# A transformer layer on one core: the feed-forward part started step by step of its contraction

## The chip, the cores and the metric

The kernel runs on one core of a Trainium2 chip. The metric is the device time of one execution in microseconds. A core has five engines, each with an instruction queue of its own that runs in order: TensorE (PE in the profile) multiplies matrices, VectorE (DVE), ScalarE (ACT) and GpSimd (POOL) work elementwise, SyncE (SP) issues DMAs; ACT issues DMAs here as well. Data lies in HBM (DRAM scratch arrays end in `_scr`), in SBUF (128 partitions) and, as matmul results, in eight PSUM banks.

## The reference

One layer over 2048 tokens of width 1024. A mixer (latent attention and a state-space part side by side) gives `y_lat`; then the feed-forward part, with d_ff = 2816:

```
x = layer_norm(DN_ALPHA * x + g1 * y_lat, ln1_g, ln1_b)
u = layer_norm(x) * (1 + sc2) + sh2                      # modulate
gate, up = split(u @ w_gate_up)                          # 1024 -> 2 x 2816
f = (silu(gate) * up) @ w_down                           # 2816 -> 1024
x = layer_norm(DN_ALPHA * x + g2 * f, ln2_g, ln2_b)
```

All of it is float32.

## The kernel before

**Precision.** A float32 product is three matmuls (`mm3`, L63 to L65): each operand is split into a rounded high part `hi` (a cast, `hi_of` L53 or an ACT copy) and the rest `lo` (`lo_of` L58, a subtraction), and hi·hi, hi·lo and lo·hi are added up in one PSUM bank.

**Stages.** Inputs and projections, attention, the `Out` stage (output product, first layer norm, second norm, and a turn that puts tokens on the free axis), then the feed-forward part: gate and up from about 1887 us, down from about 2776 us, and the end at 3318.

**Out** walks over 16 tiles of 128 tokens in time slots. For a tile: L1433 adds the residual (`xo`, DVE), statistics (L1409, DVE), L1439 normalises (ACT), L1440 and L1441 scale and shift (POOL), statistics again, L1451 makes the second norm `no` (ACT), eight transposes (L1461, PE) and eight ACT copies (L1464, `u2o`) that apply scale and shift, and a DMA to `u2_scr`. The order inside `Out` is written out by hand; after its end a scheduler merges what follows by its own costs.

**Gate and up** is one level of Strassen-Winograd: seven products in place of eight. A block is one of 22 slices f of d_ff for one of two token halves b: 7 products x 4 contraction steps k x 3 matmuls = 84 matmuls. `tokens(b)` prepares the token operands B11, B12, B21, B22 and their combinations T1 to T4 for k = 0 to 3: four loads from `u2_scr` (L1582), four DVE combinations (L1583 to L1586), seven hi casts (L1551, ACT) and seven lo (L58, DVE). They stay in SBUF for 22 blocks, as 28 pairs `oh`/`ol`. `weights(f)` does the same for one slice of weights (A11 to A22, S1 to S4): casts on POOL (L53), lo and combinations (L1565 to L1568) on DVE. `block(b, f)` runs product after product, four k each, and evacuates banks between them.

**Down** takes the tokens in four quarters q, the output columns in two halves. `hidden(q)` loads the 22 hidden slices (`hraw`, DMAs on ACT's queue, L1638) and splits them (hi on POOL). `down` runs 22 x 4 tiles x 3 matmuls per half, its weights loaded on SP and split on POOL and DVE. `add` and `finish` apply g2, the residual and the last norm; for q < 3 half of `finish` is on POOL (L1683, L1684).

The pairs `oh`/`ol` of `tokens` and `hidden` share one pool of 28, and the weights of products 0 to 3 have one buffer each, so a later use waits for PE's last read of the earlier one.

Of the kernel before, what the change touches and what calls it, by code (L numbers as in the profile page):

```python
# [10 lines left out]
F32 = mybir.dt.float32  # L11
# [1200 lines left out]
def preload(tc, E, rawp):  # L1212
    nc = tc.nc
    P = nc.gpsimd
    I = E.I
    E.after = ExitStack()
# [3 lines left out]
    E.wg = [(wp.tile([128, S5W], F32R, name="glh%d" % k), wp.tile([128, S5W], F32R, name="gll%d" % k)) for k in range(4)]  # L1220
# [93 lines left out]

class Out:
    def __init__(self, tc, E):

        self.tc, self.E = tc, E
        nc = self.nc = tc.nc
        I = E.I  # L1320
        self.cp = E.after.enter_context(tc.tile_pool(name="ou_c", bufs=2, side="right", reuse_waits="tile"))
        rows = E.after.enter_context(tc.tile_pool(name="ou_g", bufs=1, side="right", reuse_waits="tile"))
        self.att, self.s5, self.loaded = {}, {}, {}
        E.wo.append((rows.tile([128, D], F32R, name="woh7"), rows.tile([128, D], F32R, name="wol7")))
        self.operands(0)
        for k in range(4):
            self.att_load(0, k)
            self.att_part(0, k)
        self.rows = rows
        self.sh2 = rows.tile([128, 8], F32, name="sh2")  # L1330
        nc.sync.dma_start(self.sh2, E.mod_scr[1].rearrange("(k p) -> p k", p=128))
        self.sc2 = rows.tile([128, 8], F32, name="sc2")
        nc.sync.dma_start(self.sc2, E.mod_scr[2].rearrange("(k p) -> p k", p=128))
        nc.vector.tensor_scalar(self.sc2, self.sc2, 1.0, None, ALU.add)
# [46 lines left out]
    def run(self):  # L1381
# [66 lines left out]
        def second_end(t, m):  # L1448
# [19 lines left out]
        def slot(t):  # L1468
# [26 lines left out]
            turns = {2: [], 3: [0], 4: [1], 5: [2, 3]}.get(t, [b] if mb else [])  # L1495
# [35 lines left out]

class FeedForward:
    def __init__(self, tc, E, wp):

        self.tc, self.nc, self.E, self.I, self.wp = tc, tc.nc, E, E.I, wp
        self.wgu = E.I["w_gate_up"][0].rearrange("(k p) n -> p k n", p=128)

    def pair(self, pool, name, bufs=None):

        hi = pool.tile([128, 512], F32R, name=name + "h", bufs=bufs)  # L1540
        lo = pool.tile([128, 512], F32R, name=name + "l", bufs=bufs)
        return hi, lo

    def wpair(self, i):

        return self.pair(self.wp if i < 4 else self.wq, "w" + PRODUCTS[i][1], 1)

    def split(self, eng, t, raw):
# [5 lines left out]
        lo_of(self.nc.vector, lo, raw, hi)  # L1554

    def weights(self, f):
# [3 lines left out]
        r = {n: self.wp.tile([128, 512], F32, name="wraw", bufs=8) for n in ("A11", "A21", "A22", "A12", "S1", "S2", "S3", "S4")}  # L1560
# [8 lines left out]
        for _, n, _ in PRODUCTS:  # L1569
            self.split(P, w[n], r[n])  # L1570
        return w

    def tokens(self, b):

        nc, V = self.nc, self.nc.vector
        u = {n: [self.pair(self.op, "o") for _ in range(4)] for _, _, n in PRODUCTS}
        for k in range(4):
            r = {n: self.tp.tile([128, 512], F32, name="uraw", bufs=8) for n in ("B11", "B12", "B22", "B21", "T1", "T2", "T3", "T4")}
            for n in ("B11", "B12", "B22", "B21"):
# [3 lines left out]
            V.tensor_tensor(r["T1"], r["B12"], r["B11"], ALU.subtract)  # L1583
            V.tensor_tensor(r["T2"], r["B22"], r["T1"], ALU.subtract)
            V.tensor_tensor(r["T3"], r["B22"], r["B12"], ALU.subtract)
            V.tensor_tensor(r["T4"], r["T2"], r["B21"], ALU.subtract)  # L1586
            for _, _, n in PRODUCTS:
                self.split(nc.scalar, u[n][k], r[n])
        return u

    def block(self, b, f, w, u):

        nc, V, P = self.nc, self.nc.vector, self.nc.gpsimd
        tp = self.tp
# [22 lines left out]
        u3 = tp.tile([128, 512], F32, name="u3")  # L1617
        V.tensor_tensor(u3, bank["b"], s1, ALU.add)
        c22 = tp.tile([128, 512], F32, name="c22")
# [4 lines left out]
        col = b * 1024  # L1624
        nc.scalar.dma_start(self.E.h_scr[f * 128:(f + 1) * 128, col:col + 512], g1)
# [4 lines left out]
        nc.scalar.dma_start(self.E.h_scr[f * 128:(f + 1) * 128, col + 512:col + 1024], c22)  # L1630

    def hidden(self, q):

        hs = []
        for f in range(NFB):
            t = self.pair(self.op, "o")
            raw = self.bp.tile([128, 512], F32, name="hraw", bufs=6)
            self.nc.scalar.dma_start(raw, self.E.h_scr[f * 128:(f + 1) * 128, q * 512:(q + 1) * 512])  # L1638
            self.split(self.nc.gpsimd, t, raw)
            hs.append(t)  # L1640
        return hs

    def down(self, pd, tiles, half, hs, staged=0):
# [4 lines left out]
        for fs in [range(f, f + 1) for f in range(NFB - staged)] + end:  # L1648
            ws = {}
            for f in fs:  # L1650
                ws[f] = self.wpair(f % 7)
                raw = self.wp.tile([128, 512], F32, name="wraw", bufs=8)
                nc.sync.dma_start(raw, self.I["w_down"][0, f * 128:(f + 1) * 128, o])
                self.split(nc.gpsimd, ws[f], raw)
            ft = [(f, i) for i in tiles for f in ws] if len(fs) > 1 else [(f, i) for f in ws for i in tiles]
# [4 lines left out]
    def add(self, r2, st2, pd, tiles, half):  # L1660
        V = self.nc.vector
        o = slice(half * 512, (half + 1) * 512)
        for i in tiles:
            t = self.bp.tile([128, 512], F32, name="dt_", bufs=2)
            V.tensor_tensor(t, pd[i], self.g2[:, o], ALU.mult)
            V.scalar_tensor_tensor(r2[:, i, o], r2[:, i, o], ALPHA, t, ALU.mult, ALU.add)
            V.bn_stats(st2[:, i, half], r2[:, i, o])

    def finish(self, q, r2, st2, tiles):
        nc, E, sm, lg, lb = self.nc, self.E, self.sm, self.lg, self.lb  # L1670
        V, P = nc.vector, nc.gpsimd
        for i in tiles:
            r = r2[:, i, :]
# [4 lines left out]
            if q < 3:  # L1678
                nb = sm.tile([128, 1], F32, name="nb", tag="nb")
                V.tensor_scalar(nb, mv[:, 0:1], rs, -1.0, ALU.mult, ALU.mult)  # L1680
                nc.scalar.activation(r, r, AF.Identity, bias=nb, scale=rs)
                for h, e in ((slice(0, 512), P), (slice(512, 1024), V)):
                    e.tensor_tensor(r[:, h], r[:, h], lg[:, h], ALU.mult)  # L1683
                    e.tensor_tensor(r[:, h], r[:, h], lb[:, h], ALU.add)  # L1684
                nc.sync.dma_start(out, r)
            else:
                for h, e in ((slice(0, 512), V), (slice(512, 1024), P if i == 2 else V)):
                    if e is V:
                        V.scalar_tensor_tensor(r[:, h], r[:, h], mv[:, 0:1], lg[:, h], ALU.subtract, ALU.mult)
                        V.scalar_tensor_tensor(r[:, h], r[:, h], rs, lb[:, h], ALU.mult, ALU.add)  # L1690
                    else:
                        P.tensor_scalar(r[:, h], r[:, h], mv[:, 0:1], rs, ALU.subtract, ALU.mult)
                        P.tensor_tensor(r[:, h], r[:, h], lg[:, h], ALU.mult)
                        P.tensor_tensor(r[:, h], r[:, h], lb[:, h], ALU.add)
                    nc.sync.dma_start(out[:, h], r[:, h])

    def run(self):
        tc, nc, E, I = self.tc, self.nc, self.E, self.I
        with ExitStack() as st:
            self.wq = st.enter_context(tc.tile_pool(name="ff_v", bufs=2, side="right", reuse_waits="tile"))  # L1700
            self.op = st.enter_context(tc.tile_pool(name="ff_o", bufs=28, reuse_waits="tile"))
            self.sm = st.enter_context(tc.tile_pool(name="ff_s", bufs=4, reuse_waits="tile"))
            self.ps = st.enter_context(tc.tile_pool(name="ff_p", bufs=2, space=PSUM, reuse_waits="tile"))
            with tc.tile_pool(name="ff_t", bufs=2, reuse_waits="tile") as self.tp:
                w = self.weights(0)
                u = self.tokens(0)
                for b in range(2):
                    if b:
                        u = self.tokens(b)
                    for f in range(NFB):  # L1710
                        nxt = self.weights((f + 1) % NFB) if b == 0 or f + 1 < NFB else None
                        self.block(b, f, w, u)
                        w = nxt
            self.bp = bp = st.enter_context(tc.tile_pool(name="ff_b", bufs=1, reuse_waits="tile"))
            hs = self.hidden(0)
            self.g2 = row_bcast(nc, bp, E.mod_scr[3:4, :], "g2b")
            self.lg = row_bcast(nc, bp, I["ln2_g"], "l2g")
            self.lb = row_bcast(nc, bp, I["ln2_b"], "l2b")
            for q in range(4):
                r2 = bp.tile([128, 4, D], F32, name="r2")  # L1720
                nc.scalar.dma_start(r2, E.x1_scr[q * 512:(q + 1) * 512, :].rearrange("(i p) d -> p i d", p=128))
                st2 = self.sm.tile([128, 4, 2, 6], F32, name="st2", tag="st2", bufs=2)
                pd = [self.ps.tile([128, 512], F32, name="pd", tag="p" + n) for n in "abcd"]
                self.down(pd, range(4), 0, hs, 4)
                self.add(r2, st2, pd, range(4), 0)
                pd = [self.ps.tile([128, 512], F32, name="pd", tag="p" + n) for n in "abcd"]
                nxt = None
                for tiles in ((0, 1, 2, 3),) if q < 3 else ((0, 1), (2, 3)):
                    self.down(pd, tiles, 1, hs, 4 if q < 3 else 6 if 3 in tiles else 0)
                    if q < 3:  # L1730
# [122 lines left out]
```

## Time and profile before

| | us |
|---|---|
| median of 3 runs (lowest, highest) | 3314.99 (3313.58, 3319.28) |
| the profiled execution | 3319.84 |
| its span in the trace | 3318.0 |

| engine | busy, share of the span |
|---|---|
| PE | 93% |
| DVE | 68% |
| POOL | 48% |
| ACT | 36% |

The profiled execution lies 1.84 us above its span and 4.85 us above the median. The granted clock over the whole span is 0.97 of full. A busy share is a mean over stages with different limits: where PE is full, the number of matmuls sets the time; where it isn't, something else is late. The views below are read for the stretches that the change touches.

### The profile page before, as it was taken

Reading aid. Unit: us, or ns where it says so; the run is one execution under the profiler, and the core shown is the slowest. Engines: PE = TensorE matmul, PEld = TensorE weight load, DVE = VectorE, ACT = ScalarE, POOL = GpSimd, SP = SyncE. Lnnn points to the kernel's source line nnn. Section 1 sums busy time; section 2 is a strip of 40 time slices with the busy share of each in tenths; the row PEclk is TensorE's granted clock in tenths of the full one; section 3 lists DMA queues with packets and bytes.
Section 4 is the critical chain, followed back from the end, with each engine's and each line's share of the span. In section 5 each row is a group of like instructions: output and inputs, shape, how many; then the busy total and the mean of one; then the engine's idle time right before and its main releaser. Section 6 shows DMA issues by size and latency. Waiting matters only on the chain.

```text
span 3318.0 us, 47918 instructions
## 1 busy us (share of the span) xinstructions
PE 3100.5 (93%) x16693; PEld 2614.7 (79%) x16693; DVE 2267.9 (68%) x3912; ACT 1185.1 (36%) x2263; POOL 1600.7 (48%) x2429
## 2 busy tenths in 40 slices
PE   7899999999999999999778699999999998999997
PEld 4788877988988988988657478888788887777776
DVE  7755456888888767787489666656756656667556
ACT  2333354777776666666345510001100000000000
POOL 4765324877877999743244222222222225345333
PEclk9999998999999999999889899999999999999998
DMA  7444563110111222212867432223322226445434
GB/s 236 159 151 130 180 220 116 32 29 24 34 30 26 70 71 79 88 50 54 220 166 201 133 98 80 80 86 92 95 83 76 85 85 229 157 161 177 148 130 130
DMA packets 363314, 372.68 MB, mean 112 GB/s; under 512 B 95864, under 2 KB 268984, under 8 KB 363072
## 3 DMA queue, kind: packets, MB, share of 16 engines
q1 hardware_dynamic: 280720, 270.60, 27.8%
q10 hardware_dynamic: 82352, 99.02, 8.9%
q8 instruction: 131, 2.15, 0.3%
q14 instruction: 111, 0.91, 0.1%
HBM read 269.24 MB, written 100.29 MB: 111 GB/s over the span
## 4 chain that ended last, share of the span: by engine, by line
PE 59%; POOL 8%; DVE 7%; issue 6%; DMA 3%; ACT 1%; SPq 0%; POOLq 0%; ACTq 0%; DVEq 0%
PE tps L1022 6%; PE pd L64 4%; PE pd L63 4%; PE pd L65 4%; PE O L1046 3%; PE O L1045 3%; PE pa L64 2%; PE pa L63 2%; PE pb L63 2%; PE pb L64 2%; PE pb L65 2%; PE pa L65 2%; PE pc L63 2%; PE pc L64 2%; PE pc L65 2%
## 5 line engine op out<-in xcount | busy, mean ns | idle before, releaser
L1033 DVE TENSOR_TENSOR ptl<-tps,pth 128x512 fp32r<-128x512 f32 x576 | 380.3, 685 | 100.3 <-ACT pth L1027 99.9
L1027 ACT CAST pth<-tps 128x512 fp32r<-128x512 f32 x576 | 336.5, 587 | 158.6 <-PE tps L1022 134.3
L1045 PE MATMUL O<-pth,vhl 128*128 128x256 f32 x1152 | 322.7, 304 | 0.6 <-DVE oo L1054 0.6
L1046 PE MATMUL O<-ptl,vhl 128*128 128x256 f32 x1152 | 297.9, 282 | 2.1 <-DVE ptl L1033 1.7
L999 DVE TENSOR_REDUCE mx<-SB 128x1 f32<-128x1280 f32 x128 | 190.7, 1490 | 77.7 <-PE SB L65 77.7
L1046 PEld LDWEIGHTS O<-ptl,vhl 128*128 128x128 f32 x1152 | 219.7, 191 | 10.3 <-DVE ptl L1033 3.5
L1045 PEld LDWEIGHTS O<-pth,vhl 128*128 128x128 f32 x1152 | 217.9, 189 | 7.7 <-ACT pth L1027 1.1
L1628 ACT ACTIVATE u<-u 128x512 f32<-128x512 f32 x44 | 27.8, 632 | 517.6 <-DVE u L1627 517.6
L1022 PE MATMUL tps<-ident,PB 128*128 128x128 f32 x1280 | 192.5, 272 | 4.8 <-DVE ptl L1033 4.8
L1010 ACT ACTIVATE PB<-SB,nm 128x1280 f32<-128x1280 f32 x128 | 170.7, 1334 | 4.8 <-DVE nm L1004 4.8
L1022 PEld LDWEIGHTS tps<-ident,PB 128*128 128x128 f32 x1280 | 152.1, 140 | 24.1 <-DVE ptl L1033 7.6
L999 DVE TENSOR_REDUCE mx<-SA 128x1 f32<-128x1024 f32 x128 | 156.0, 1219 | 18.2 <-PE SA L65 17.9
L73 ACT ACTIVATE rq_s<-rq_v 128x1 f32<-128x1 f32 x68 | 12.7, 200 | 395.3 <-DVE rq_v L71 392.9
L1022 PE MATMUL tps<-ident,PA 128*128 128x128 f32 x1024 | 152.0, 273 | 1.6 <-DVE ptl L1033 1.4
L63 PE MATMUL SB<-kh,qh 96*128 96x512 f32 (+1 forms) x384 | 145.7, 379 | 0.0
L1010 ACT ACTIVATE PA<-SA,nm 128x1024 f32<-128x1024 f32 x128 | 143.5, 1121 | 5.3 <-DVE nm L1004 5.3
L774 POOL TENSOR_TENSOR sct<-scan_tab,hist 128x128 f32<-128x128 f32 x286 | 132.8, 464 | 24.5 <-ACT hist L763 4.9
L58 DVE TENSOR_TENSOR ol<-hraw,oh 128x512 fp32r<-128x512 f32 x88 | 92.2, 1066 | 71.5 <-POOL oh L53 71.5
L65 PE MATMUL SB<-kh,ql 96*128 96x512 f32 (+1 forms) x384 | 138.5, 361 | 0.0
L64 PE MATMUL SB<-kl,qh 96*128 96x512 f32 (+1 forms) x384 | 138.0, 359 | 0.0
L1022 PEld LDWEIGHTS tps<-ident,PA 128*128 128x128 f32 x1024 | 121.3, 141 | 12.8 <-DVE ptl L1033 2.3
L53 POOL TENSOR_SCALAR oh<-hraw 128x512 fp32r<-128x512 f32 x88 | 66.2, 759 | 120.6 <-PE pd L64 100.5
(534 smaller groups left out, 9886.1 us busy)
## 6 DMA issues: line engine op xcount, KB each, us to landing
wraw<-in_w_down SPq DMA_DIRECT2D x198, 256.0 KB
wraw<-in_w_gate_up SPq DMA_DIRECT2D x176, 256.0 KB
hraw<-h_scr ACTq DMA_DIRECT2D x88, 256.0 KB
wad<-in_w_ada SPq DMA_DIRECT2D x32, 512.0 KB
h_scr<-g ACTq DMA_DIRECT2D x44, 256.0 KB
h_scr<-c ACTq DMA_DIRECT2D x44, 256.0 KB
wada<-in_w_ada SPq DMA_DIRECT2D x16, 512.0 KB
xt<-in_x SPq DMA_DIRECT2D x16, 512.0 KB
```

The costliest lines, as they stand in the source:

```text
L58: eng.tensor_tensor(lo, raw, hi.bitcast(F32), ALU.subtract)
L63: nc.tensor.matmul(out, sh, mh, start=first, stop=False, skip_group_check=onto)
L64: nc.tensor.matmul(out, sh, ml, start=False, stop=False, skip_group_check=onto)
L65: return nc.tensor.matmul(out, sl, mh, start=False, stop=last, skip_group_check=onto)
L774: nc.gpsimd.tensor_tensor(t, E.scan_tab, hist[:, i:i + 1].broadcast_to([128, 2, 2, 2, G // 2]), ALU.mult)
L999: nc.vector.reduce_max(mx, SB if u else SA, axis=AX.X)
L1010: nc.scalar.activation(ex, SB if u else SA, AF.Exp, bias=hd.nm[:, u, t:t + 1], scale=SCALE, accum_out=hd.sums[:, u, t:t + 1])
L1022: nc.tensor.transpose(ps[:, kk, j * 128:(j + 1) * 128], pr.P[(j, u)][:, o:o + 128], ident)
L1027: nc.scalar.copy(hi, pr.pt[g][0])
L1033: nc.vector.tensor_tensor(lo, ps, hi.bitcast(F32), ALU.subtract)
L1045: nc.tensor.matmul(o, vk, hi[:, kk, :], start=k in (0, 8), stop=False)
L1046: nc.tensor.matmul(o, vk, lo[:, kk, :], start=False, stop=k in (7, 17))
```

## The change

It touches the feed-forward part and the end of `Out`.

1. `first` computes the block b = 0, f = 0 with the contraction step outermost: for each k all seven products, in seven PSUM banks, and the elementwise work behind all of them. The other blocks stay as they were.
2. The last two tiles of `Out` (14 and 15) are not turned there: ACT writes `no` to a new scratch `n_scr`, and `late` loads, turns and stores them behind blocks f = 4 and f = 5.
3. `tokens` takes its pairs step by step in the order of use, makes T2, T3, T4 in place in the buffers of B11, B12 and B21 (five raw tiles a step, not eight), and for b = 0 gives two lo of a step to POOL.
4. `weights` makes S3, S2, S4 in place, with 6 raw buffers and not 8. The pairs of products 4 to 6 rotate in a pool of four that exists since before `Out`.
5. `hidden` loads on SP and casts on ACT. For q = 0 it runs in the last block of gate and up and in the first half of down; for q + 1 slice by slice within the second half of q.
6. The residual of down is eight tiles loaded on SP at f = 8 to 11, not one tile on ACT's queue. `finish` normalises and stores by halves.
7. `sh2` and `sc2` and the pools lie in other places; the rows g2b, l2g and l2b get a home at the start of gate and up.

```diff
+STEP = (0, 2, 6, 3, 4, 1, 5)
...
     def weights(self, f):
...
+        r["S3"] = r["A21"]
+        V.tensor_tensor(r["S3"], r["A11"], r["A21"], ALU.subtract)
+        self.split(P, w["A11"], r["A11"])
+        r["S2"] = r["A11"]
         V.tensor_tensor(r["S2"], r["S1"], r["A11"], ALU.subtract)
-        V.tensor_tensor(r["S3"], r["A11"], r["A21"], ALU.subtract)
+        for n in ("S2", "A12", "S1", "S3", "A22"):
+            self.split(P, w[n], r[n])
+        r["S4"] = r["A12"]
...
     def tokens(self, b):
...
+            def part(n):
+                self.split(nc.scalar, t[n], r[n], nc.gpsimd if b == 0 and n in ("B21", "T3") else None)
+
+            part("B11")
             V.tensor_tensor(r["T1"], r["B12"], r["B11"], ALU.subtract)
+            part("B21")
+            part("B22")
+            part("T1")
+            r["T3"] = r["B12"]
+            V.tensor_tensor(r["T3"], r["B22"], r["B12"], ALU.subtract)
+            part("T3")
...
+    def first(self, b, f, w, u):
+
+        nc, V = self.nc, self.nc.vector
+        bank = [self.ps.tile([128, 512], F32, name="p" + n) for n in "abacbdc"]
+        for k in range(4):
+            sl = slice(k * 128, (k + 1) * 128)
+            for i in STEP:
+                wh, wl = w[PRODUCTS[i][1]]
+                mm3(nc, bank[i], wh[:, sl], wl[:, sl], *u[PRODUCTS[i][2]][k], k == 0, k == 3)
...
+    def late(self, i):
+
+        nc, E = self.nc, self.E
+        t = NLAT // 128 - LATE + i
+        for b in range(2):
+            n = self.up.tile([128, 512], F32, name="uraw", bufs=8)
+            nc.sync.dma_start(n, E.n_scr[i, :, b * 512:(b + 1) * 512])
+            pt = self.ps.tile([128, 512], F32, name="pd")
+            for q in range(4):
+                nc.tensor.transpose(pt[:, q * 128:(q + 1) * 128], n[:, q * 128:(q + 1) * 128], E.ident)
...
+    def hidden(self, q, f):
+
+        t = self.pair()
+        raw = self.up.tile([128, 512], F32, name="uraw", bufs=8)
+        self.nc.sync.dma_start(raw, self.E.h_scr[f * 128:(f + 1) * 128, q * 512:(q + 1) * 512])
+        self.split(self.nc.scalar, t, raw)
+        return t
...
     def run(self):
...
+                    (self.block if b or f else self.first)(b, f, w, u)
                     w = nxt
+                    if b == 0 and 4 <= f < 4 + LATE:
+                        self.late(f - 4)
...
+            for g in range(4):
+                hs.append(self.hidden(0, g))
```

How the instructions stand now. ACT at the end of `Out`, before, from the second norm of tile 14 (first `no`) on; `u2o` are the turn's copies and the `oh` casts are those of `tokens(0)`:

```order
L1451 ACTIVATE no<-xo,rb,rr 128x1024
L1439 ACTIVATE xo<-xo,rb,rr 128x1024
L1464 ACTIVATE u2o<-pt,sh_20807,sc_20809 128x128 x8
L1445 DMA x_scr<-xo 128x1024
L1466 DMA u_scr<-u2o 128x8x128
L1413 ACTIVATE sd<-bmv,eps 128x1
L1451 ACTIVATE no<-xo,rb,rr 128x1024
L1464 ACTIVATE u2o<-pt,sh_20807,sc_20809 128x128 x8
L1466 DMA u_scr<-u2o 128x8x128
L1551 CAST oh<-uraw 128x512 x22
```

The same place now (L1442, L1454 and L1564 are the lines that were L1439, L1451 and L1551):

```order
L1454 ACTIVATE no<-xo,rb,rr 128x1024
L1442 ACTIVATE xo<-xo,rb,rr 128x1024
L1458 DMA n_scr<-no 128x1024
L1448 DMA x_scr<-xo 128x1024
L1416 ACTIVATE sd<-bmv,eps 128x1
L1454 ACTIVATE no<-xo,rb,rr 128x1024
L1564 CAST oh<-uraw 128x512 x5
L1458 DMA n_scr<-no 128x1024
L1564 CAST oh<-uraw 128x512 x20
```

The casts stand right behind the last `no`. The same end of `Out` on DVE, before, around the residual add of tile 15 (`xo<-xo,py`):

```order
L58 TENSOR_TENSOR wS3l<-wraw,wS3h 128x512
L58 TENSOR_TENSOR wA22l<-wraw,wA22h 128x512
L58 TENSOR_TENSOR wS4l<-wraw,wS4h 128x512
L1566 TENSOR_TENSOR wraw<-wraw 128x512
L1567 TENSOR_TENSOR wraw<-wraw 128x512
L1583 TENSOR_TENSOR uraw<-uraw 128x512
L1568 TENSOR_TENSOR wraw<-wraw 128x512
L1584 TENSOR_TENSOR uraw<-uraw 128x512
L1585 TENSOR_TENSOR uraw<-uraw 128x512
L1586 TENSOR_TENSOR uraw<-uraw 128x512
L1433 SCALAR_TENSOR_TENSOR xo<-xo,py 128x1024
```

and now (L1436 and L1412 were L1433 and L1409):

```order
L1412 BN_STATS bst<-xo 128x6 x2
L1414 BN_AGGR bmv<-bst 128x2
L1436 SCALAR_TENSOR_TENSOR xo<-xo,py 128x1024
L1422 RECIPROCAL rr<-sd 128x1
L1412 BN_STATS bst<-xo 128x6 x2
```

The ten feed-forward instructions are gone from in front of the add. Weight instructions stand earlier in `Out` (14 there now, 9 before), the token combinations behind the last norm. Third place: POOL where the first quarter of down ends, before (the `w` and `oh` are casts of weights and hidden slices, L1683 and L1684 belong to `finish`):

```order
L53 TENSOR_SCALAR oh<-hraw 128x512
L53 TENSOR_SCALAR wS3h<-wraw 128x512
L53 TENSOR_SCALAR oh<-hraw 128x512
L1683 TENSOR_TENSOR r_30385<-r_30385,l2g 128x512
L53 TENSOR_SCALAR wA22h<-wraw 128x512
L1684 TENSOR_TENSOR r_30385<-r_30385,l2b 128x512
L53 TENSOR_SCALAR wA11h<-wraw 128x512
```

and now (L1768, L1769 were L1683, L1684; `gh` are rotating weight pairs, `w0h` was `wA11h`):

```order
L53 TENSOR_SCALAR w3h<-wraw 128x512
L53 TENSOR_SCALAR gh<-wraw 128x512
L1768 TENSOR_TENSOR s<-s,l2g 128x512
L53 TENSOR_SCALAR gh<-wraw 128x512
L1769 TENSOR_TENSOR s<-s,l2b 128x512
L53 TENSOR_SCALAR w0h<-wraw 128x512
```

The hidden casts have left this queue for ACT's.

## Rows read from the trace of the kernel before

**Rows 1.** Busy time and clock by stretch: columns as in its head; steady block loop.

```profile
core 0: us, PE busy (x) PEld busy (x) DVE busy (x) ACT busy (x) POOL busy (x), PEclk, DMA share, GB/s
2000.00:2100.00 100.00, 100.00 (x437) 81.74 (x436) 61.11 (x94) 9.64 (x17) 25.09 (x37) 1.00 0.28 83
```

**Rows 2.** The same view, from `Out`'s end into the first blocks.

```profile
1880.00:1890.00 10.00, 4.86 (x14) 3.64 (x15) 3.44 (x8) 7.71 (x16) 0.00 (x0) 0.50 0.44 124
1890.00:1900.00 10.00, 6.57 (x20) 3.17 (x19) 9.20 (x16) 4.44 (x9) 0.00 (x0) 0.97 0.56 162
1900.00:1910.00 10.00, 6.04 (x16) 3.06 (x17) 9.85 (x17) 6.19 (x12) 1.64 (x1) 0.88 0.47 154
1910.00:1920.00 10.00, 10.00 (x36) 7.96 (x35) 6.96 (x12) 3.72 (x6) 3.69 (x5) 0.78 0.44 135
1920.00:1930.00 10.00, 9.85 (x43) 7.70 (x42) 9.48 (x16) 0.00 (x0) 2.20 (x3) 1.00 0.12 36
```

**Rows 3.** DVE in order of time: start, us, instruction, idle before and its releaser.

```profile
1860.76 0.81 DVE L58 TENSOR_TENSOR wS3l<-wraw,wS3h 128x512 fp32r<-128x512 f32 x1
...
1866.91 1.21 DVE L1433 SCALAR_TENSOR_TENSOR xo<-xo,py 128x1024 f32<-128x1024 f32 x1
...
1892.19 0.69 DVE L1583 TENSOR_TENSOR uraw<-uraw 128x512 f32<-128x512 f32 x1 [0.80 <-DMA uraw<-u_scr]
...
1898.82 0.69 DVE L1583 TENSOR_TENSOR uraw<-uraw 128x512 f32<-128x512 f32 x1
```

**Rows 4.** PE in order of time: its first matmul of the feed-forward part.

```profile
1887.10 0.80 PE L63 MATMUL pa<-oh,wA11h 128*128 128x512 f32 x1 [3.21 <-ACT oh L1551]
```

**Rows 5.** The chain that ended last, 1845 to 1913: start, us, what.

```profile
1845.80 0.66 PE pt L1461 x4
...
1880.63 1.25 ACT no L1451
...
1886.43 0.63 ACT oh L1551
...
1887.81 4.26 DMA uraw<-u_scr
...
1912.85 0.43 PE pb L65
```

**Rows 6.** One line of `finish` on both engines: ns min/median/max, first and last start.

```profile
L1684 DVE TENSOR_TENSOR r<-r,l2b x12: 684/1630/1780, 2904.4 to 3185.8; 128x512 f32<-128x512 f32 x12
L1684 POOL TENSOR_TENSOR r<-r,l2b x12: 1259/1606/1719, 2906.5 to 3185.3; 128x512 f32<-128x512 f32 x12
```

**Rows 7.** Busy time by stretch, where the second token half begins.

```profile
2325.00:2355.00 30.00, 24.25 (x79) 17.21 (x78) 24.84 (x40) 9.09 (x17) 4.54 (x7) 0.83 0.31 95
```

**Rows 8.** Busy time by stretch, start of down and three quarter boundaries.

```profile
2740.00:2790.00 50.00, 38.87 (x159) 31.21 (x159) 27.16 (x36) 2.45 (x4) 19.49 (x25) 0.86 0.59 195
2890.00:2940.00 50.00, 45.03 (x186) 36.19 (x185) 39.38 (x70) 6.96 (x9) 31.11 (x30) 0.93 0.52 174
3020.00:3070.00 50.00, 45.03 (x189) 36.45 (x188) 39.48 (x71) 5.57 (x8) 31.34 (x30) 0.93 0.51 171
3150.00:3200.00 50.00, 45.28 (x187) 36.61 (x186) 35.76 (x65) 5.57 (x8) 25.64 (x25) 0.93 0.46 158
```

**Rows 9.** PE's waits, 2740 to 3318: us in total, times, longest.

```profile
PE pd L63 <- POOL wA11h L53: 20.9, 8, 5.0
PE pd L63 <- POOL oh L53: 11.1, 1, 11.1
```

**Rows 10.** POOL and ACT's queue in order of time, at the start of down.

```profile
2775.59 0.62 POOL L53 TENSOR_SCALAR oh<-hraw 128x512 fp32r<-128x512 f32 x1 [9.98 <-DMA hraw<-h_scr]
...
2767.70 29.15 ACTq L1638 DMA_DIRECT2D hraw<-h_scr  x22
```

**Rows 11.** POOL, then DVE, in order of time, at the first quarter boundary.

```profile
2903.26 1.05 POOL L53 TENSOR_SCALAR oh<-hraw 128x512 fp32r<-128x512 f32 x1
...
2907.76 1.06 POOL L53 TENSOR_SCALAR wA11h<-wraw 128x512 fp32r<-128x512 f32 x1
...
2909.69 0.82 DVE L58 TENSOR_TENSOR wA11l<-wraw,wA11h 128x512 fp32r<-128x512 f32 x1
```

More of the change, by code (lines that the diff above doesn't have):

```diff
@@ L1215, in preload @@
     I = E.I
+    E.gp = E.st.enter_context(tc.tile_pool(name="pairs", bufs=4, side="right", reuse_waits="tile"))
     E.after = ExitStack()
@@ L1329, in __init__ @@
         self.rows = rows
[L1330 to L1334, printed above, removed]
+        nc.sync.dma_start(E.sh2, E.mod_scr[1].rearrange("(k p) -> p k", p=128))
+        nc.sync.dma_start(E.sc2, E.mod_scr[2].rearrange("(k p) -> p k", p=128))
+        nc.vector.tensor_scalar(E.sc2, E.sc2, 1.0, None, ALU.add)
     def rows_load(self):
@@ L1559, in weights @@
         w = {p[1]: self.wpair(i) for i, p in enumerate(PRODUCTS)}
-        r = {n: self.wp.tile([128, 512], F32, name="wraw", bufs=8) for n in ("A11", "A21", "A22", "A12", "S1", "S2", "S3", "S4")}
+        r = {n: self.wp.tile([128, 512], F32, name="wraw", bufs=6) for n in ("A11", "A21", "A22", "A12", "S1")}
         for n in ("A11", "A21", "A22", "A12"):
@@ L1629, in block, with down @@
         V.tensor_tensor(c22, c22, u2, ALU.mult)
[L1630 to L1643, printed above, removed]
+        self.store(b, f, 1, c22)
+    def late(self, i):
[7 more added lines that the diff above has]
+                nc.tensor.transpose(pt[:, q * 128:(q + 1) * 128], n[:, q * 128:(q + 1) * 128], E.ident)
+            u2 = self.up.tile([128, 512], F32, name="uraw", bufs=8)
+            for q in range(4):
+                k = b * 4 + q
+                nc.scalar.activation(u2[:, q * 128:(q + 1) * 128], pt[:, q * 128:(q + 1) * 128], AF.Identity,
+                                     bias=E.sh2[:, k:k + 1], scale=E.sc2[:, k:k + 1])
+            nc.scalar.dma_start(E.u2_scr[b * 512:(b + 1) * 512, t * 128:(t + 1) * 128].rearrange("(k p) t -> p k t", p=128),
+                                u2.rearrange("p (k t) -> p k t", k=4))
+    def hidden(self, q, f):
[4 more added lines that the diff above has]
+        return t
+    def down(self, pd, tiles, half, hs, staged=0, ahead=None):
         nc = self.nc
@@ L1680, in finish @@
                 V.tensor_scalar(nb, mv[:, 0:1], rs, -1.0, ALU.mult, ALU.mult)
[L1681 to L1695, printed above, removed]
+            for half in range(2):
+                r = r2[i][half]
+                h = slice(half * 512, (half + 1) * 512)
+                if q < 3:
+                    nc.scalar.activation(r, r, AF.Identity, bias=nb, scale=rs)
+                    e = V if half else P
+                    e.tensor_tensor(r, r, lg[:, h], ALU.mult)
+                    e.tensor_tensor(r, r, lb[:, h], ALU.add)
+                elif half and i == 2:
+                    P.tensor_scalar(r, r, mv[:, 0:1], rs, ALU.subtract, ALU.mult)
+                    P.tensor_tensor(r, r, lg[:, h], ALU.mult)
+                    P.tensor_tensor(r, r, lb[:, h], ALU.add)
+                else:
+                    V.scalar_tensor_tensor(r, r, mv[:, 0:1], lg[:, h], ALU.subtract, ALU.mult)
+                    V.scalar_tensor_tensor(r, r, rs, lb[:, h], ALU.mult, ALU.add)
+                nc.sync.dma_start(out[:, h], r)
     def run(self):
@@ L1702, in run @@
+            self.ob = st.enter_context(tc.tile_pool(name="ff_q", bufs=4, side="right", reuse_waits="tile"))
+            self.rows = st.enter_context(tc.tile_pool(name="ff_r", bufs=1, reuse_waits="tile"))
             self.sm = st.enter_context(tc.tile_pool(name="ff_s", bufs=4, reuse_waits="tile"))
             self.ps = st.enter_context(tc.tile_pool(name="ff_p", bufs=2, space=PSUM, reuse_waits="tile"))
[L1704 to L1713, printed above, removed]
@@ new lines, in run @@
+            u = self.tokens(0)
+            for b in range(2):
+                if b:
+                    u = self.tokens(b)
+                for f in range(NFB):
+                    nxt = self.weights((f + 1) % NFB) if b == 0 or f + 1 < NFB else None
+                    (self.block if b or f else self.first)(b, f, w, u)
+                    w = nxt
+                    if b == 0 and 4 <= f < 4 + LATE:
+                        self.late(f - 4)
+            self.g2 = row_bcast(nc, self.rows, E.mod_scr[3:4, :], "g2b")
@@ new lines, in run, with early, beside @@
+            self.lg = row_bcast(nc, self.rows, I["ln2_g"], "l2g")
+            self.lb = row_bcast(nc, self.rows, I["ln2_b"], "l2b")
+            hs, nxt = [], []
+            def early(f):
+                for g in range(4 * f, min(4 * f + 4, NFB)):
+                    hs.append(self.hidden(0, g))
+            for g in range(4):
+                hs.append(self.hidden(0, g))
+            for q in range(4):
+                if q:
+                    hs, nxt = nxt, []
+                r2 = {}
+                def beside(f):
+                    if q == 0:
+                        early(f + 1)
+                    if 8 <= f < 12:
+                        i = f - 8
+                        r2[i] = [self.tile("r2") for _ in range(2)]
+                        for half in range(2):
+                            nc.sync.dma_start(r2[i][half], E.x1_scr[q * 512 + i * 128:q * 512 + (i + 1) * 128, half * 512:(half + 1) * 512])
@@ L1722, in run @@
                 st2 = self.sm.tile([128, 4, 2, 6], F32, name="st2", tag="st2", bufs=2)
[L1723 to L1724 removed]
+                pd = [self.ps.tile([128, 512], F32, name="p" + n) for n in "abcd"]
+                self.down(pd, range(4), 0, hs, 4, beside)
                 self.add(r2, st2, pd, range(4), 0)
[L1726 removed]
@@ L1777, in build @@
         nc.vector.memset(E.eps, EPS)
+        E.sh2 = kc.tile([128, 8], F32, name="sh2")
+        E.sc2 = kc.tile([128, 8], F32, name="sc2")
         E.scan_tab = kc.tile([128, 2, 2, 2, G // 2], F32, name="scan_tab")
```

120 lines of the change are left out of this document (73 added, 47 removed).

## The prediction

> **What bounds the kernel now.** I read the busy time by stretch first, because the change touches four places of one long stage. In the steady block loop PE is busy 100.00 of 100 us at full clock with 437 matmuls [rows 1]: one matmul is 100/437 = 0.2288 us, and DVE (61), POOL (25) and ACT (10) are covered. Nothing outside PE can gain there, and no matmul is saved: the change leaves 44 blocks of 84 and 2112 matmuls of down, and moves 16 transposes. What can be gained is the time in which PE is not full. The same view shows four such places: the start of the first block [rows 2], the start of the second token half [rows 7], the start of down and the three quarter boundaries [rows 8]. The order in time, the chain and the waits say what is late at each. I price each place as matmuls missing against 0.2288 us, which counts stalls and lowered clock together.
>
> **a. The end of Out and the first block.** By 1930 us PE has done (14 - 8 transposes) + 20 + 16 + 36 + 43 = 121 block matmuls [rows 2]. At full pace they would have started at 1930 - 121 x 0.2288 = 1902.3. I call that the virtual start; the change gains what it moves it forward.
>
> What is late is the chain of tile 15. DVE has ten feed-forward instructions in front of its residual add, from 1860.76 to 1866.91 [rows 3], 0.615 us each; the change takes them away, so the add starts 6.15 us earlier, at 1860.76. From the add to the start of the last norm are 1880.63 - 1866.91 = 13.7 us, and the norm takes 1.25 [rows 3, 5]; behind it stood the eight transposes and copies of the turn, and now stands a cast of 0.63 us. So the first matmul comes at 1860.76 + 13.7 + 1.25 + 0.63 = 1876.4 in place of 1887.10 [rows 4]. Against that, five more weight instructions (14, not 9) stand earlier in Out: 5 x 0.615 = 3.1 us if DVE sets the time there, nothing if it idles; I take the middle, 1.5. First matmul 1877.9.
>
> From there the tokens set the time. Before, a step of k took 1898.82 - 1892.19 = 6.63 us, which is 11 DVE instructions at 0.60 with DVE all but full [rows 2, 3]. Now DVE has nine (two lo are POOL's): 9 x 0.615 = 5.5 us if POOL does not disturb it. But a subtraction of 128x512 on DVE takes 0.68 us alone and 1.63 in the median while POOL does one of its own, and POOL's takes 1.26 to 1.7 [rows 6]. So each POOL lo costs DVE about 0.95, and a step is 5.5 + 2 x 0.95 = 7.4 us: longer than before. I take 7.4, as the row nearest to it is an instruction of the same shape; 5.5 is one end. The loads may lie bare as well: one takes 4.26 us, and DVE already waited 0.80 for one [rows 3, 5]. In their favour a step now holds five raw buffers of eight, not eight; against them the three row broadcasts (512 KB each) now lie between them on SP's queue. As the other end I add 1.5 us a step.
>
> What turns this into a gain is PE. It runs all 21 matmuls of a step, 21 x 0.2288 = 4.8 us, inside the step, where before it ran four products (12 matmuls) and had the other 36 still to do. By the order of the changed kernel 89 matmuls stand in front of the one that reads the last lo, five of them block 1's. The last lo lands at 1877.9 + 4 x 7.4 = 1907.5, and the virtual start is 1907.5 - 89 x 0.2288 = 1887.1: a gain of 15.2. The 16 transposes of the late turns come back inside full blocks: 4 take 0.66 us [rows 5], so 2.6 us are lost. Their 16 copies lie on ACT, which is free there, and their loads are issued a block ahead. Net **12.5 us**. Ends: with steps of 5.5 us the last lo lands at 1899.9 and the net gain is 20; with 8.9 (7.4 + 1.5) it is 6.6.
>
> **b. The second token half.** 79 matmuls ran in 30 us where 131 fit: 52 x 0.2288 = 11.9 us are lost [rows 7]. DVE is busy 24.84 of the 30: its 28 lo and 16 combinations remain (none goes to POOL for b = 1), so this stays bound by DVE. The change can fill only DVE's idle 5.2 us, by loads that come earlier (free buffers sooner) and combinations that go out in the order in which pairs are needed. I take 3; ends 0 and 6.
>
> **c. The start of down.** 159 matmuls in 50 us where 218.5 fit: 13.6 us lost [rows 8], of which 11.1 are one wait for POOL's first hidden cast [rows 9]. That cast stood idle 9.98 us for a load which ACT's queue issued at 2767.70, behind the last block [rows 10]. Now the first four slices, and more as raw buffers and pairs come free, are loaded on SP and cast on ACT within the last block, for columns that were stored half the stage ago. The price of the new wait (a cast waits for PE to let go a pair of `tokens`) is hidden: PE frees them product by product through a block of 84 x 0.2288 = 19.2 us. I take 13; ends 5 (only the stall's first half goes, if loads queue behind weights on SP) and 13.6.
>
> **d. Quarter boundaries.** 186, 189 and 187 matmuls where 218.5 fit: 32.5, 29.5 and 31.5 lost, 7.1 us each in the mean [rows 8]. PE waits for `wA11h` (20.9 us in eight waits, the longest 5.0) [rows 9]: POOL's queue has hidden casts (1.05 us) and `finish` in front of it [rows 11]. Two such casts leave the queue there: 2 x 1.05 = 2.1 us earlier. But the third matmul also wants the lo, which DVE makes at 2909.69, behind `finish` [rows 11], and nothing there has moved; POOL's fewer casts let DVE go faster a little. I take 1.4 each, 4 in all; ends 0 and 8 (2.1 plus some of the lowered clock, three times). The half boundaries and the last quarter keep their waits.
>
> The rest I price at nothing: the in-place combinations, 6 raw buffers and rotating pairs of `weights` (cover: PE's other products, see the second rival), the residual on SP (needed only at the end of a half, some 14 slices of 12 matmuls after its load), the hoisted `sh2`, `sc2`.
>
> **Sum.** 12.5 + 3 + 13 + 4 = 32.5 us off the profiled execution's 3319.84, or 3287.3. The median of the runs lies 4.85 lower, so I forecast 3314.99 - 32.5 = **3282.5 us**.
>
> **Rivals.**
>
> *The first block gains little.* The gain in a rests on PE keeping full clock while it waits at every step. Before, in the stretch 1890 to 1900, PE was busy 6.57 of 10 and the granted clock was 0.97; in the next it was 6.04 and 0.88, then 0.78 [rows 2], and a matmul took 0.43 us where the clock was halved [rows 5]. If the first block ran all at that pace, a step would be 21 x 0.43 = 9.0 us, its end 1877.9 + 36.1 = 1914 and the virtual start 1914 - 84 x 0.2288 = 1894.8; the net gain is 7.5 - 2.6 = 4.9 and the time 3290. For it: the dips in rows 2. Against it: pairs come every 0.8 to 1 us and each feeds 0.69 us of matmuls, so the waits are short and spread. The Trainium skill, in "TensorE: Matmul & The Clock Gate" (HAM oscillation), speaks against this change: a loop that waits for data at each contraction step is throttled anew at each step, and it advises running all steps of one tile before the next wait, which is what the kernel did. By that rule the time would be this rival's; the row with 0.97 at 6.57 busy does not bear it out, the following ones do in part.
>
> *The steady loop gets a new wait (slower).* S2, S3 and S4 now overwrite A11, A21 and A12, and 6 raw buffers serve where 8 did, so a slice's loads can only start when the chain of casts of the one before is through. One slice's chain is at most seven casts at 1.06 and seven lo at 0.82 [rows 11], 13.2 us, and a load 4.26: 17.4 of the 19.2 us that a block takes. If it slips, each of 43 blocks pays: at 32.5/43 = 0.76 us a block the whole gain is gone, at 1.5 us the time is 3314.99 - 32.5 + 64.5 = 3347. For it: the margin is 1.8 us by these upper bounds. Against it: those are durations beside a busy DVE; the loop's POOL is busy 25 of 100, and the casts of the next slice start when its product ends, not at the end of the block.
>
> *The start of down moves its wait.* Hidden loads stand in SP's queue among weights; if the fifth and later slices come late, PE waits there piecewise. Then c is 5 and the time 3290.5.
>
> *The boundaries and the first block do better*: POOL's lo do not slow DVE, or the clock holds at the boundaries. Then a is 20 or d is 8, and the time 3271 to 3278.
>
> **How the numbers follow.** The forecast with its own range of 3276 to 3289: 0.50. First block weak: 0.17. Down's wait moved: 0.08. Better: 0.13. Steady wait: 0.12, of which 0.02 still leaves a gain, 0.04 about nothing and 0.06 a loss. The range is 3266 to 3300: it takes in the sum of the upper ends less a little (20 + 6 + 13.6 + 8 = 47.6, not all at once) and the first block and down's start both weak (3314.99 - 4.9 - 3 - 5 - 2). A measurement of this kernel tells 0.2%, 6.6 us, from no change. Faster by more: 0.90. Within it: 0.04. Slower: 0.06, from the steady wait alone.
>
> **What would show it.** In the changed profile: the first block matmul near 1878, with no turn in front; DVE's instructions at 1.5 us and more beside POOL's in the first block, a step of about 7.4 us, and PE doing all seven products in it; about 437 matmuls per 100 us in blocks, without new waits; the gap at the second half nearly as long; no stall at the start of down; POOL's first weight cast two places earlier at a boundary with PE then waiting for DVE. The prediction is wrong if the block loop shows fewer matmuls per 100 us, if a step in the first block is over 9 us, or if PE stalls for hidden casts at the start of down.

## The result

The changed kernel takes 3278.12 us in the median of four runs (3274.37 to 3279.64), the kernel before 3316.64 in four; the ratio is 0.9882, 95% interval 0.9865 to 0.9900. That is 38.5 us less, where 32.5 were forecast. The profiled execution took 3274.37 us, its span 3272.6. Its busy times:

```profile
PE 3075.9 (94%) x16693; PEld 2605.3 (80%) x16693; DVE 2265.0 (69%) x3906; ACT 1245.3 (38%) x2364; POOL 1566.3 (48%) x2349
```

PE does the same 16693 matmuls in 24.6 us less busy time: 3100.5 before. This was not forecast; the steady blocks show where it lies. The busy time by stretch of the changed kernel, for the end of Out, the steady loop [rows 1, 2], the second token half [rows 7], the start of down and the three quarter boundaries [rows 8]:

```profile
1870.00:1880.00 10.00, 4.54 (x11) 3.33 (x12) 7.62 (x14) 4.22 (x7) 3.31 (x3) 0.52 0.50 183
1880.00:1890.00 10.00, 7.93 (x28) 4.50 (x26) 9.82 (x13) 5.32 (x10) 3.59 (x3) 1.00 0.54 181
1890.00:1900.00 10.00, 7.15 (x25) 4.39 (x25) 9.86 (x12) 6.27 (x11) 5.24 (x3) 1.00 0.75 240
1900.00:1910.00 10.00, 7.96 (x26) 5.82 (x27) 9.49 (x12) 2.34 (x4) 6.74 (x6) 0.85 0.00 0
1910.00:1920.00 10.00, 10.00 (x43) 7.88 (x43) 9.50 (x16) 3.62 (x5) 2.49 (x4) 0.98 0.28 80
2030.00:2130.00 100.00, 100.00 (x443) 82.81 (x442) 61.76 (x94) 9.54 (x16) 26.83 (x37) 1.00 0.27 85
2310.00:2340.00 30.00, 24.43 (x84) 16.32 (x84) 27.61 (x45) 10.84 (x19) 9.61 (x7) 0.89 0.50 159
2710.00:2760.00 50.00, 48.78 (x216) 40.10 (x215) 37.58 (x56) 16.41 (x28) 15.16 (x18) 1.00 0.65 222
2852.00:2902.00 50.00, 46.09 (x193) 37.16 (x192) 37.98 (x68) 11.38 (x19) 22.68 (x21) 0.93 0.54 180
2982.00:3032.00 50.00, 46.02 (x190) 37.06 (x189) 38.33 (x67) 9.99 (x18) 24.93 (x22) 0.93 0.59 192
3111.00:3161.00 50.00, 46.00 (x196) 37.19 (x195) 36.31 (x63) 6.68 (x12) 25.45 (x24) 0.97 0.46 156
```

443 matmuls in 100 us stand against 437 [rows 1], with PE full in both. A window also counts the matmuls that reach over its edges, so dividing by the count gives a little too little. From the start of one steady block to the next it is 19.04 us for 84 matmuls and not 19.31, or 0.2267 us each and not 0.2299. The start of down has 216 in 50 us (159 before), the boundaries 190 to 196 (186 to 189). PE's first wait, and its waits in down (us in total, times, longest) [rows 4, 9]:

```profile
1875.46 0.80 PE L63 MATMUL pa<-oh,w0h 128*128 128x512 f32 x1 [16.06 <-ACT oh L1564]
```

```profile
PE pa L63 <- POOL w0h L53: 14.9, 7, 3.9
PE pa L64 <- DVE w0l L58: 3.6, 5, 1.2
```

The wait for hidden casts is gone; that for the weight at a quarter boundary fell from 5.0 to 3.9.

Counting the 5808 matmuls of gate, up and down in order of time splits the span at the same work in each kernel. The third column is the first experiment below, the kernel before with other addresses:

| from matmul, to | before | before, shifted | after |
|---|---|---|---|
| start to the first | 1887.1 | 1885.6 | 1875.5 |
| 0 to 168, two blocks | 54.7 | 54.0 | 53.8 |
| 168 to 1764, 19 blocks | 366.8 | 361.8 | 364.3 |
| 1764 to 1932, second half begins | 50.7 | 48.1 | 50.4 |
| 1932 to 3695 | 405.4 | 399.6 | 401.1 |
| 3695 to 3696, down begins | 11.5 | 12.3 | 0.2 |
| 3696 to 5800 | 528.6 | 521.1 | 514.2 |
| to the end | 13.1 | 13.2 | 13.2 |

### The profile page after: what moved, and what is told of

The parts are those of the page before. It is cut to its first block, busy times and chain, and to the rows that moved or that the text cites. A ratio compares the mean times of both kernels' runs of the same rounds, so it can differ in the third digit from the quotient of the medians.

```text
span 3272.6 us, 48053 instructions
## 1 busy us (share of the span) xinstructions
PE 3075.9 (94%) x16693; PEld 2605.3 (80%) x16693; DVE 2265.0 (69%) x3906; ACT 1245.3 (38%) x2364; POOL 1566.3 (48%) x2349
## 5 line engine op out<-in xcount | busy, mean ns | idle before, releaser
L53 POOL TENSOR_SCALAR gh<-wraw 128x512 fp32r<-128x512 f32 x217 | 182.5, 842 | 447.4 <-PE pb L64 89.2
L58 DVE TENSOR_TENSOR gl<-wraw,gh 128x512 fp32r<-128x512 f32 x213 | 155.6, 733 | 92.3 <-POOL gh L53 90.3
L1564 ACT CAST oh<-uraw 128x512 fp32r<-128x512 f32 x144 | 85.8, 619 | 331.5 <-PE pd L64 196.0
L1692 ACT ACTIVATE s<-s 128x512 f32<-128x512 f32 x43 | 27.3, 634 | 416.2 <-DVE s L1691 416.2
L58 DVE TENSOR_TENSOR ol<-uraw,oh 128x512 fp32r<-128x512 f32 x136 | 102.5, 773 | 66.3 <-ACT oh L1564 66.1
```

The source lines that it names most:

```text
L53: eng.tensor_scalar(hi, raw, 1.0, 0.0, ALU.mult, ALU.add)
L58: eng.tensor_tensor(lo, raw, hi.bitcast(F32), ALU.subtract)
```

## The experiments

**Addresses.** In the trace before, a block's seven products did not run alike: from one matmul to the next 0.2267 us in products 1 to 3, 0.2335 in 4 to 6. After, all run at 0.2267. The instructions are the same but for the operands' places: in the compiled program of before, the tokens and the weights of products 0 to 3 start at 160 modulo 256 bytes, the weights of 4 to 6 at 224; after, all are at 224, because `sh2` and `sc2` (64 bytes) moved in front of the left pools and the tokens to the right side (pools are laid out from both ends of a partition's memory; `side="right"` names the far end).

```diff
+            pp = st.enter_context(tc.tile_pool(name="ff_pad", bufs=1, reuse_waits="tile"))
+            nc.vector.memset(pp.tile([128, 16], F32, name="ff_pad"), 0.0)
             wp = st.enter_context(tc.tile_pool(name="ff_w", bufs=2, reuse_waits="tile"))
```

> The kernel before, with 64 unused bytes per partition in front of the feed-forward pools, nothing else. Theory A (a matmul takes 0.2333 us and not 0.2267 where the SBUF addresses of its stationary and its moving operand differ modulo 128 bytes; in before these are products 4 to 6 of every block and 864 of the 2112 matmuls of down; with the pad none differs): 443 matmuls per 100 us in the steady blocks, not 437; a block 19.04 us, not 19.31, so 43 blocks give 11.6 us, and down (0.2289 to 0.2268 a matmul) 4.4: about 3301. Rival B (the new kernel's shorter pitch comes from its order of work, its in-place tiles or its fewer buffers): 437 and no change, 3316.

Measured: 3296.19 us, 0.9949 of the kernel before (0.9934 to 0.9964), 15.5 us off. The steady blocks by stretch:

```profile
2040.00:2140.00 100.00, 100.00 (x442) 82.83 (x442) 60.13 (x93) 9.13 (x16) 25.66 (x37) 1.00 0.29 86
2440.00:2540.00 100.00, 100.00 (x443) 82.84 (x442) 62.70 (x99) 8.52 (x15) 25.12 (x37) 1.00 0.27 79
```

Theory A held, B fell: 64 unused bytes bring the whole of the shorter pitch (0.2267 us from one matmul to the next in all seven products). The same pad in the changed kernel:

> The changed kernel with the same 64 bytes, which shift its left pools alone: now the operands of products 0 to 3 differ modulo 128 bytes, and those of 4 to 6 still agree. Theory A: 48 to 53 of 84 matmuls at 0.2333, so about 434 per 100 us and 14 us over 43 blocks; in down the weights f modulo 7 = 0 to 3, 1200 or so of 2112 matmuls, another 8 to 9 us: about 3300. Rival B: 443 and 3278.

Measured: 3293.28 us, 0.9941 (0.9924 to 0.9958), 15 us above the changed kernel, where theory A had 22; products 0 to 3 at 0.2335, 4 a little over 0.2267, 5 and 6 at 0.2267, in the tenth block. The slow pace has moved to the products whose operands now differ.

```profile
2040.00:2140.00 100.00, 100.00 (x435) 81.51 (x434) 60.15 (x93) 9.69 (x16) 26.40 (x36) 1.00 0.25 79
```

And with `[128, 32]` for the pad's size:

> The changed kernel with 128 bytes in place of 64: the operands of products 0 to 3 agree modulo 128 and differ modulo 256. If 128 is the modulus that counts: 443 per 100 us and 3278. If it is 256 (or any shift does harm): as with 64 bytes, 434 and about 3300.

Measured: 3296.94 us, 0.9951 (0.9936 to 0.9965).

```profile
2040.00:2140.00 100.00, 100.00 (x436) 81.83 (x435) 60.44 (x94) 9.69 (x16) 26.40 (x36) 1.00 0.25 79
```

A difference of 128 costs nearly what 64 does (products 0 to 3 at 0.232 to 0.233). My modulus was wrong: agreeing modulo 128 is not enough. In the changed kernel left and right pools differ modulo 512 (224 and 480) at full pace, so agreeing modulo 256 is.

```diff
+        E.eps = kc.tile([128, 1], F32, name="eps")
+        E.sh2 = kc.tile([128, 8], F32, name="sh2")
+        E.sc2 = kc.tile([128, 8], F32, name="sc2")
         E.ident = kc.tile([128, 128], F32, name="ident")
         make_identity(nc, E.ident)
-        E.eps = kc.tile([128, 1], F32, name="eps")
...
-        E.sh2 = kc.tile([128, 8], F32, name="sh2")
-        E.sc2 = kc.tile([128, 8], F32, name="sc2")
```

> The changed kernel with three small constant tiles laid in front of the identity matrix and not behind it: the 2304 transposes of attention, whose identity stood 96 bytes (modulo 128) off the tile they transpose, now agree; nothing else shifts. Theory A in its wide form (any matmul): each transpose of four in a row shorter by up to 0.0066 us, 15 us in all if PE sets attention's time, and perhaps less of the 0.09 us by which the matmul behind them is late: 3263 or less. Rival: only streams of 512 columns are touched, no change, 3278.

Measured: 3282.79 us, 0.9911 (0.9895 to 0.9928). Attention, this kernel:

```profile
600.00:800.00 200.00, 198.47 (x1388) 181.44 (x1387) 166.86 (x250) 141.77 (x246) 149.61 (x359) 1.00 0.11 29
```

The changed kernel has 1392 matmuls there. From one transpose to the next it is 0.110 us in both. The wide form fell: the transposes don't gain. Matmuls of other widths were not tried.

**The first block.** Four kernels on one chip.

> The changed kernel again, unaltered, on the same chip as the next three: the yardstick for them. Expected 0.9882 of the kernel before, as first measured; a first-block step of 7.8, 7.8 and 6.7 us.

Measured: 3277.93 us, 0.9899 (0.9883 to 0.9916). Its first block matmul came at 1879.0, 3.6 us later than in the first trace: so much do the stages ahead vary. The steps took 7.9, 7.8 and 6.7 us, as expected.

```diff
-                self.split(nc.scalar, t[n], r[n], nc.gpsimd if b == 0 and n in ("B21", "T3") else None)
+                self.split(nc.scalar, t[n], r[n], None)
```

> The changed kernel with all lo of the first token half on DVE, none on POOL. Theory C (a POOL lo costs DVE about 1.1 us, more than the 0.60 it takes over): a step is 11 x 0.60 = 6.6 to 6.7 us in place of 7.8, over the two to three steps that were slow 2 to 4 us off the kernel. Rival (DVE bound the first block by its count: nine instructions are better than eleven): 2 x 0.6 x 4 = 4.8 us slower.

Measured: 3274.22 us, 0.9890 (0.9875 to 0.9904); from the first matmul to the end of the second block 49.9 us, 53.8 in the run before this one. In the changed kernel's trace one sees why (DVE, then POOL, in order of time): a combination beside a POOL lo takes 1.78 us, without one 0.68.

```profile
1881.43 0.68 DVE L1607 TENSOR_TENSOR uraw<-uraw 128x512 f32<-128x512 f32 x1
...
1883.83 1.78 DVE L1612 TENSOR_TENSOR uraw<-uraw 128x512 f32<-128x512 f32 x1
...
1889.23 0.68 DVE L1607 TENSOR_TENSOR uraw<-uraw 128x512 f32<-128x512 f32 x1
```

```profile
1883.28 1.79 POOL L58 TENSOR_TENSOR ol<-uraw,oh 128x512 fp32r<-128x512 f32 x1 [3.10 <-ACT oh L1564]
```

A step is 1889.23 - 1881.43 = 7.8 us. With every lo on DVE the steps began at 1875.08, 1883.73, 1890.48 and 1896.02: 8.7, 6.8 and 5.5 us. Theory C held in sign and size: 3.9 us within the trace; the intervals of the two ratios overlap, so by time alone it is not settled. DVE's slowing is not all of it. In the changed kernel PE waits 3.5 us for POOL's lo, without them not at all, and the longest of these waits is in the last step: there three casts of the next slice's weights stand ahead of the lo in POOL's queue (POOL, then PE, then DVE's last lo of the block, in the changed kernel).

```profile
1901.34 0.93 POOL L53 TENSOR_SCALAR w0h<-wraw 128x512 fp32r<-128x512 f32 x1 [1.90 <-PE pa L64]
1902.25 1.05 POOL L53 TENSOR_SCALAR w2h<-wraw 128x512 fp32r<-128x512 f32 x1
1903.26 1.05 POOL L53 TENSOR_SCALAR w3h<-wraw 128x512 fp32r<-128x512 f32 x1
1904.28 1.69 POOL L58 TENSOR_TENSOR ol<-uraw,oh 128x512 fp32r<-128x512 f32 x1
```

```profile
1906.02 0.50 PE L64 MATMUL pb<-ol,gh 128*128 128x512 f32 x1 [1.95 <-POOL ol L58]
```

```profile
1908.06 0.68 DVE L58 TENSOR_TENSOR ol<-uraw,oh 128x512 fp32r<-128x512 f32 x1
```

```diff
-                    (self.block if b or f else self.first)(b, f, w, u)
+                    (self.block if f else self.first)(b, f, w, u)
```

> As the run before, and the first block of the second token half step by step of the contraction too. Theory D (that transition is bound by DVE's 44 token instructions and some 20 others, all in 50 us; PE only waits): the loss of 12 us there stays within 2 us. Rival (product by product PE waits for the last step's pairs before it can begin the second product, so the order costs): 3 to 8 us off.

Measured: 3264.24 us, 0.9858 (0.9842 to 0.9875). From matmul 1764 to 1932 it took 42.2 us (50.1 in the run before it), but part of that is only put off: the block behind them took 22.2 us, 3.1 more than in the run before. Over the three blocks it is 64.3 us against 69.1, a gain of 4.8. The stretch, in this kernel:

```profile
2310.00:2320.00 10.00, 9.96 (x43) 7.68 (x42) 9.45 (x17) 5.50 (x11) 4.46 (x1) 1.00 0.55 178
2320.00:2330.00 10.00, 9.59 (x36) 6.05 (x35) 10.00 (x14) 3.20 (x7) 5.25 (x6) 1.00 0.50 160
```

and in the unaltered one on the same chip:

```profile
2320.00:2330.00 10.00, 7.10 (x25) 3.90 (x23) 9.49 (x17) 4.87 (x9) 4.45 (x1) 0.99 0.56 191
2330.00:2340.00 10.00, 8.99 (x25) 5.93 (x26) 9.96 (x16) 5.05 (x9) 1.35 (x2) 0.67 0.55 181
```

Theory D fell, and the rival's 3 to 8 us held. DVE is full in both, but PE, given all products of a step, is not idle for it. By time this kernel beats the unaltered one. It is also 10.0 us under the run before it, but not all of that is the order's: of the 12.7 us by which the two profiled spans differ, 7.2 lie ahead of the first block matmul (1869.8 against 1877.0), where the kernels are alike.

```diff
-                    (self.block if b or f else self.first)(b, f, w, u)
+                    self.block(b, f, w, u)
```

> The changed kernel with the first block product by product, as before; tokens, late turns and all else as changed. My prediction's account: the 36 matmuls of products 4 to 6 come behind the last step and not inside it, less the block 1 matmuls that fill: 5 to 8 us slower. Rival (from the first matmul to the end of the second block both kernels take 54 us, so the order in PE gains nothing and all of the gain at the start is the earlier first matmul): within 2 us of the changed kernel.

Measured: 3280.53 us, 0.9908 (0.9893 to 0.9923); two blocks take 58.3 us against 53.8. The order in PE is worth 4.5 us by the trace, a little less than my account's 5 to 8 and more than the rival's 2; by time, 2.6 us, it is not settled. The stretch:

```profile
1880.00:1890.00 10.00, 7.79 (x16) 4.51 (x17) 9.91 (x14) 6.09 (x11) 3.81 (x3) 0.67 0.69 224
1890.00:1900.00 10.00, 7.81 (x18) 4.30 (x17) 9.88 (x12) 4.86 (x9) 4.81 (x3) 0.67 0.62 193
```

Product by product PE did 16 and 18 matmuls in these stretches, where the changed kernel did 28 and 25, and the granted clock was 0.67 against 1.00. So low a clock does not always come with that order: the kernel before, product by product too, had 0.97 and 0.88 [rows 2].

**The start of down and the turns.**

```diff
-            self.nc.scalar.dma_start(raw, self.E.h_scr[f * 128:(f + 1) * 128, q * 512:(q + 1) * 512])
+            self.nc.sync.dma_start(raw, self.E.h_scr[f * 128:(f + 1) * 128, q * 512:(q + 1) * 512])
```

> The kernel before with the loads of hidden issued by SP and not by ACT, one line. My prediction's account of the 11.1 us stall at the start of down (ACT's queue issues the first load only at 2767.7, behind the last block's store): the load leaves SP early and the stall is gone or under 3 us. Rival (the load waits for memory: its raw tile lies in a pool that takes over the space of the block loop's tiles, so it can start on no queue before the last block has ended): a stall of 8 to 12 us stays, and the kernel with it.

Measured, in one run: 3319.15 us, which tells nothing by time: the kernel before took 3309.76 to 3319.18 on that chip. The stall is 7.6 us (PE's waits, then SP's queue):

```profile
PE pd L63 <- POOL oh L53: 7.6, 1, 7.6
```

```profile
2745.59 22.43 SPq L1653 DMA_DIRECT2D wraw<-in_w_down  x9
2768.43 30.91 SPq L1638 DMA_DIRECT2D hraw<-h_scr  x21
```

Neither account gave this. The load again leaves at 2768, now behind nine loads for weights that wait for buffers; in the compiled program the first one waits for no memory that is still in use, only for earlier DMAs. So I read it as the place in a queue, as I had it, but another queue does not mend it; no run shows the load leaving earlier by this alone. In the changed kernel SP issues eight hidden loads far ahead, before the weights of the following blocks:

```profile
2326.05 10.49 SPq L1718 DMA_DIRECT2D uraw<-h_scr  x8
```

Which of its edits lets them go so early (the shared raw pool, or the code's order) wasn't tried.

```diff
-LATE = 2
+LATE = 0
```

> The changed kernel with all sixteen turns at the end of Out, as before; the rest as changed. My prediction's account: the first cast waits for eight transposes and eight copies behind the last norm (before: 1880.63 + 1.25 to 1886.43, 4.5 us), and 2.6 us of transposes leave blocks 4 and 5: 2 us slower in all, the first block matmul 4 to 5 us later against the end of Out. Rival (the ten feed-forward instructions on DVE stand in front of tile 15's add because of the turns: they return): 6 us more, 8 us slower.

Measured: 3284.10 us, 0.9914 (0.9897 to 0.9930), on another chip than the yardstick, so not to be told from it by time. In the trace two blocks take 58.1 us (53.8 with late turns), and the three blocks from the fifth on lose the transposes (matmul 336 to 588: 57.1 us and not 59.3). The first matmul must be counted from the residual add of tile 15, since the stages ahead vary. First the add in the changed kernel (its first matmul is at 1875.46), then the add and the first matmul in this one:

```profile
1860.03 1.20 DVE L1436 SCALAR_TENSOR_TENSOR xo<-xo,py 128x1024 f32<-128x1024 f32 x1
```

```profile
1858.97 1.21 DVE L1436 SCALAR_TENSOR_TENSOR xo<-xo,py 128x1024 f32<-128x1024 f32 x1
1876.10 0.78 PE L63 MATMUL pa<-oh,w0h 128*128 128x512 f32 x1
```

The first matmul comes 17.1 us behind the add without late turns, 15.4 with them, 20.2 in the kernel before. So it is 1.7 us later, not 4 to 5, and the other 4.3 us are lost in the two blocks: the last turn's copies now stand among the first casts. Less the 2.2 us of transposes, the late turns are worth 3.8 us by the trace, where I had 2. The ten instructions did not return in front of the add.

## Why the prediction was right, and where it was not

The time lay within the range, 4.4 us from the forecast, and part of that is luck: one term was missing and two were too large. Against the shifted kernel, whose matmuls run at the same pace, the changed one gains 3295.7 - 3272.6 = 23.1 us of span, where my sum had 32.5; the rest, 22.3 of span and 15.5 of the medians, is addresses. These are spans of single executions; by the ratios (0.9949 with the pad, 0.9882 and 0.9899 changed) the change's own part is 17 to 22 us. With mismatched operands in it the changed kernel took 3293.28 and 3296.94, some 11 to 14 us above the forecast: it was a gain that I had not seen which brought the time so near.

- "No matmul is saved", "nothing outside PE can gain there", the new places in memory priced at nothing: this step failed. (The 0.2288 us of a matmul also came from a count that takes in the edges of its window; by starts it was 0.2299.) PE 100.00 busy [rows 1] does not say that a matmul takes its least time; products 4 to 6 took 3% more, and the first experiment shows why.
- **a**, 12.5 forecast, 7.9 found (10.1 to the first matmul, 0.3 in two blocks, less 2.5 in the 19 blocks with the late turns). Counted from Out's first residual add, the first matmul comes at 225 and 226 us in the two traces of the changed kernel, at 236 in the traces of the kernel before and the shifted one: the 10 us are not chance. The first matmul at 1875.5 and 1879.0 (1877.9 forecast), DVE's 1.78 beside POOL and the step of 7.8 (7.4 forecast) were right. The last step was not: from 1895.93 to the end of its last lo it took 12.8 us, as the next slice's weights, which my step had no room for, stand between its instructions on DVE and POOL. So the last lo came 33.3 us behind the first matmul, not 4 x 7.4 = 29.6. And I mis-sized what PE's order brings: 4.5 us, and POOL's lo, which come with it, cost 3.9. So two blocks take 53.8 us against 54.0.
- **b**, 3 forecast, -2.3 found. I took DVE's count for the bound and looked for the gain in its idle time; DVE idles less, and PE stands as long. What was to be had lay in PE's order: 4.8 us, by the run that has both first blocks step by step.
- **c**, 13 forecast: 12.1 at the first matmul of down, and 3.0 in the half behind it (63.9 to 60.9 us), where the clock no longer falls; less 1.5 us lost in the blocks ahead, the last of which now holds the casts: 13.6.
- **d**, 4 forecast: 514.2 against 521.1 is 6.9, of which 3.0 are c's: 3.9. The longest wait is 3.9, not 5.0: 1.1 us at each, near the 1.4 argued. This is the best case: in the second trace of the changed kernel the same matmuls took 516.7, which leaves 1.4. No run tests d by itself.
- The rivals. A first block at a fallen clock did not come: 0.52 at its very start, then 1.00 for 20 us, 0.85 after a wait of 1.95 for a POOL lo. The Trainium skill's advice to run all steps of a tile before the next wait ("TensorE: Matmul & The Clock Gate", HAM oscillation) is given for a loop whose wait for data is longer than a step's matmuls. Here the longest wait within a step is 1.95 us, the 21 matmuls of a step take 4.8, and the traces do not bear the advice out: with all products of one step at hand the clock held, with one product after the other it was 0.67 in one kernel and 0.97 and 0.88 in another. The steady loop has no new wait: in-place combinations and six raw buffers cost nothing that the trace shows. Down's wait did not move.

## What to carry to other kernels

A full PE can still be slow: take the time from the start of one matmul to the next, product by product, and where like instructions differ, compare the operands' addresses. Where operands become ready step by step and DVE is full, give PE all products of a step; here that hid 4.5 us of waits and lowered clock in one place and 4.8 in another, and what is hidden can come back in the next block: count that one too. Handing one of two SBUF-fed subtractions to POOL cost DVE 1.1 us here, to save it 0.60.

## What was not expected of the hardware

A float32r matmul of 128x512 follows the one before it after 0.2267 us where its two operands' start addresses agree modulo 256 bytes, and after 0.232 to 0.2335 where they differ by 64 or 128; other differences were not tried. One pad of 64 bytes was worth 0.5% of the kernel (ratio 0.9949, 0.9934 to 0.9964). The slow pace lingers: in the trace before, the first product of the next block began at 0.23 to 0.236 though its operands agree. Why is open. The 128-column transposes showed no such effect.
